# Four gate rows by way of DRAM instead of TensorE, and a written order at the end of the first MLP

## The chip, the cores and the metric

The kernel runs on one core of a Trainium2 chip. The metric is the device time of one execution in microseconds. A core has TensorE (PE, with its weight loads shown apart as PEld), VectorE (DVE), ScalarE (ACT) and GpSimd (POOL), which run their own instruction streams and wait for each other by semaphores, and SyncE (SP), whose stream here issues nearly all DMAs. DMAs move data between DRAM and the on-chip memory SBUF; matmul results arrive in the accumulator memory PSUM.

## The reference

Two layers of a diffusion backbone over 512 latent tokens and 256 context tokens, width 1024, hidden width 4096. Layer 0 mixes tokens by pooling, layer 1 by attention; each layer has an MLP with squared ReLU. Cut to what matters here:

```python
def ada_mods(cond, w, b):
    m = (jax.nn.silu(cond) @ w + b)[..., None, :]
    return jnp.split(m, N_MOD, axis=-1)
...
    for i in range(DEPTH):
        last = i == DEPTH - 1
        sh1, sc1, gt1, sh2, sc2, gt2 = ada_mods(c, w_ada[i], b_ada[i])
        csh1, csc1, cgt1, csh2, csc2, cgt2 = ada_mods(c_ctx, w_ada[i], b_ada[i])
        ...
        x = x + gt1 * rms_norm(y_lat, g_mix_post[i])
        m_lat = sq_relu_mlp(modulate(rms_norm(x, g_mlp_pre[i]), sh2, sc2), w_mlp_in[i], w_mlp_out[i])
        x = x + gt2 * rms_norm(m_lat, g_mlp_post[i])
        if not last:
            ctx = ctx + cgt1 * rms_norm(y_ctx, g_mix_post[i])
            ...
            ctx = ctx + cgt2 * rms_norm(m_ctx, g_mlp_post[i])
    return x
```

A gate, `gt1` or `gt2`, is one vector of 1024 numbers for all latent tokens and another for all context tokens. The kernel multiplies it with the gain of the norm behind it and applies it to rows of tokens.

## The kernel before

Tokens lie in six row tiles of 128: tiles 0 to 3 are latent, 4 and 5 context. Matmul operands are split into a high and a low float32r part, and a product is three matmuls (high by high, high by low, low by high).

**Two layouts of a gate.** The modulations come out as columns: number 128k + p of a vector sits in partition p, column k. The rows of tokens need the vector along the free axis, the same in all 128 partitions: the tile `gate`, [128, 2, 1024], slot 0 for latent rows and slot 1 for context rows. There are six such turns of a column into a row: one in two halves (`gate_half`) and one whole (`gate_rows`) early in layer 0, two in `before0`, one in the attention and one behind the last MLP. `gate_cols` (line 363) makes the column by one small VectorE multiply. `gate_rows` (line 373) turns it with eight float32 matmuls of the broadcast column by the identity, each recorded as two, and two ScalarE copies of PSUM. `gate_diag` (line 383) splits the column into two parts, has VectorE multiply the identity by each ([128, 8, 128], into tiles named diag), and sums over partitions with four matmuls against a column of ones, then copies on ScalarE. PSUM tiles of both are named psg and come from the pool `psB` (four banks), which out-products and transposes use too.

**The first MLP** (`mlp0`, line 1074) runs over 16 groups of 256 hidden channels on all 768 tokens. From the third group, an in-product is done with seven block products instead of eight (`Seven`, line 854): chains 0 to 6 of twelve matmuls each in the PSUM tile psin, chain 4 with the sums S3 and T3, chain 6 last. Between chains, ACT copies a bank or VectorE adds one, and the next chain on that bank waits. Each group's out-product (`out_mm`, line 1028, PSUM tile pso) adds into the token rows. For the last two groups it is done together in `finish` (line 1063), row tile by row tile in the order 4, 5, 0, 1, 2, 3, with 24 matmuls a tile: 12 of the older group, 12 of the newer. `last0` (line 1405) puts the norm, gate, residual and next norm of each tile behind it, and `norm_pair` turns two tiles at a time with 16 transposes (PSUM tile psx) for the projections (psq) of the attention. The context pair 4 and 5 is the first to be turned.

**Around it.** `mid0` and `extra0` (lines 1249 and 1258) run between and in the groups and compute the other modulations, on VectorE. `before0` (line 1449), behind the last in-product, closes the pool of sums, opens the pool of resident rows in its place (`xr`, `gate`, `junk`, `xl`), makes the two gates of layer 0's MLP by `gate_diag` and reloads the six row tiles from the DRAM tile `spill`. In the attention's list of steps `gate_rows` for layer 1's first gate stands at 39.281; the second MLP (`mlp1`, line 1101) ends with `residents` again, reloads and `finish`, with `gate_diag` for the last gate at 5.1.

**What sets the order.** The tile framework schedules the program with a simulated timeline (line 38), so instructions of one engine are ordered by program order, readiness and simulated times; DMAs too. A list of steps with times (`Steps`) sets the program order. `pin` and `tc.add_manual_dep` with `ISSUE` add an edge without a semaphore: the first must be issued behind the second. Regions of SBUF are handed out by pools, so another set of tiles shifts addresses. DMAs are issued on SP in the scheduled order, and a DMA that waits holds those behind it.

Of the kernel before, what the change touches and what calls it, by code (L numbers as in the profile page):

```python
# [9 lines left out]
F32 = mybir.dt.float32  # L10
# [43 lines left out]
def backbone(ctx: ExitStack, tc, x, c, ctx_in, c_ctx, w_ada, b_ada, g_mix_pre, g_mix_post,  # L54
# [53 lines left out]
    def residents(stack):  # L108
        rows = Rows(stack)
        return rows, rows.gate, rows.junk  # L110
# [2 lines left out]
    psA = ctx.enter_context(tc.tile_pool(name="psA", bufs=2, space=PSUM))  # L113
    psB = ctx.enter_context(tc.tile_pool(name="psB", bufs=4, space=PSUM))
    spill = ctx.enter_context(tc.tile_pool(name="spill", bufs=1, space=bass.MemoryType.DRAM)).tile([P, NT, D], F32, name="spill")

    acc = const.tile([P, NT * D], F32, name="acc")
    ident = const.tile([P, P], F32, name="ident")
# [261 lines left out]
                pin(z, i == 0 and m == GT1)  # L380
            sc.copy(gate[:, ci, 512 * h:512 * h + 512], ps)

    def gate_diag(i, m, ci, to=None):
        to = ci if to is None else to
        gc = gate_cols(i, m, ci)
        gh = small.tile([P, 2, KT], F32R, tag="gh", name="gh", bufs=2)
        ve.tensor_copy(gh[:, 0, :], gc)
        ve.tensor_tensor(out=gh[:, 1, :], in0=gc, in1=gh[:, 0, :], op=ALU.subtract)
        dg = [tmp.tile([P, KT, P], F32R, tag="t", name="diag") for _ in range(2)]
        for z, d in enumerate(dg):  # L390
            ve.tensor_tensor(out=d, in0=ident.unsqueeze(1).broadcast_to([P, KT, P]),
                             in1=gh[:, z, :].unsqueeze(2).broadcast_to([P, KT, P]), op=ALU.mult)
        for h in range(2):
            ps = psB.tile([P, 512], F32, tag="b", name="psg")
            for z, d in enumerate(dg):
                te.matmul(ps, onesr[:, 0:1].broadcast_to([P, P]), d[:, 4 * h:4 * h + 4, :], start=(z == 0), stop=(z == 1))
            sc.copy(gate[:, to, 512 * h:512 * h + 512], ps)

    def gate_half(h):
        gc = sm_tile("gc")  # L400
# [23 lines left out]

    late = []

    def modulated_pair(t, i, s, hi, lo, works, wide, fine, on_act):
        if (i, s) == (0, 1):
            place = lambda z, ks: z.rearrange("p k (h q n) -> p k q h n", h=2, n=P)[:, ks, t // 2]
# [6 lines left out]
        for q in range(4):  # L436
            if not wide:
                ps = psB.tile([P, 2, 256], F32, tag="b", name="psx")
            elif q % 2 == 0:
                both = psA.tile([P, 4, 256], F32, tag="a", name="psx")  # L440
            if wide:
                ps = both[:, 2 * (q % 2):2 * (q % 2) + 2, :]
            for kk in range(2):
                k = 2 * q + kk
                for u in range(2):
                    te.transpose(ps[:, kk, u * P:(u + 1) * P], works[u][:, k * P:(k + 1) * P], ident)
            pss.append(ps)
        for q in range(4):
            h = works[q // 2][:, 512 * (q % 2):512 * (q % 2) + 512].rearrange("p (k n) -> p k n", n=256)
# [403 lines left out]

    class Seven:
        def __init__(self, products, hid):
            self.products = products
            self.a, self.ntok = (hH, hL), TOK
            self.hid = [z.rearrange("p (f n) -> p f n", n=TOK) for z in hid]

        def chain(self, bank, n, start, stop):  # L860
            (wH, wL), (aH, aL) = self.products[n]
            for k in range(4):
                for m, (w, a) in enumerate(((wH, aH), (wH, aL), (wL, aH))):
                    te.matmul(bank, w[k], a[k], start=start and k == 0 and m == 0, stop=stop and k == 3 and m == 2,
                              skip_group_check=True)
# [159 lines left out]

    pso = {}

    def out_mm(i, parts, t, cols=HALVES):
# [11 lines left out]
        seq = [(a, f, w) for (_, (hi, lo), (wH, wL)) in parts for f in range(2)  # L1040
               for a, w in ((hi, wH), (hi, wL), (lo, wH))]
        order = [(n, h) for n in range(len(seq)) for h in range(len(cols))]
        if len(parts) > 1:
            order.sort(key=lambda z: (z[0] >= (9 if cols == HALVES else 0), z[1]))
        for n, h in order:
            a, f, w = seq[n]
            te.matmul(pss[h][:, 0:cols[h][1]], a[:, f, ts_], w[:, f, cols[h][0]:sum(cols[h])],
                      start=(n == 0 and not seeded[t]), stop=(n == len(seq) - 1), skip_group_check=seeded[t])
        pso[t] = pss

    def out_ev(i, parts, t, cols=HALVES):
# [11 lines left out]
    def finish(i, parts, order, last, also=()):  # L1063
        st = Steps()
        for z in also:
            st.at(*z)
        for n, t in enumerate(order):
            cols = THIRDS if (i, t) == (1, NL - 1) else HALVES
            st.at(5.2 * n, out_mm, i, parts, t, cols)
            st.at(5.2 * n + 5.2, out_ev, i, parts, t, cols)  # L1070
            last(st, n, t)
        st.run()

    def mlp0(inner, hids, order, extra, mid, last, before_last):
# [7 lines left out]
        for g in range(NG - 1):  # L1082
# [11 lines left out]
            else:  # L1094
                for t in range(NT):
                    out_mm(0, [part], t)
                    out_ev(0, [part], t)
        before_last()
        finish(0, [part, (NG - 1, inner.hid, wo_)], order, last)

    def mlp1(inner, last):
        nonlocal xr, gate, junk
# [66 lines left out]
        for p in range(NG // 2 - 1):  # L1169
# [29 lines left out]
            inner = inner_of(2 * p + 2)  # L1199
            if p == 1:  # L1200
                ada_fin(1, GT2, parts[1], 1)
        whole = lambda n: tuple(z.rearrange("p (f n) -> p f n", f=2) for z in (home[n], home[n + 1]))
        half_ = lambda n: (home[n][:, 0:1024], home[n][:, 1024:2048])
        wo_ = []
# [20 lines left out]
                add(m7_, m7_, m5)  # L1225
        closing.close()
        xr, gate, junk = residents(ctx)
        for t in range(NL):
            sy.dma_start(xr[:, t], spill[:, t])
        finish(1, [(NG - 2 + q, last_[q].hid, wo_[q]) for q in range(2)], range(NL), last, ((5.1, gate_diag, 1, GT2, 0),))  # L1230

    dual = [(0, GT2, 2), (1, SC1, 2), (1, SH1, 2)]
    lone = [(1, m, 1) for m in (GT1, SC2, SH2)]
# [359 lines left out]
    def attention(st, base, unit_t):  # L1593
# [127 lines left out]
```

## Time and profile before

| | before |
|---|---|
| median of 3 executions | 1157.09 us (1157.08 to 1157.51) |
| the profiled execution | 1157.33 us |
| its span | 1155.2 us |
| PE busy | 1134.3 us (98%), 6026 matmuls |
| PE weight loads busy | 979.8 us (85%) |
| DVE busy | 938.0 us (81%), 1551 instructions |
| ACT busy | 644.8 us (56%), 1150 instructions |
| POOL busy | 74.4 us (6%), 82 instructions |
| DMA | 152.08 MB, mean 132 GB/s |

The span goes from the first to the last instruction; the time of an execution holds 2.1 us more. Matmuls are pipelined and their ends are modelled, so a matmul of 128x512 is recorded with a length of 392 ns though in a run of many one starts every 0.23 us. Helpers record every operation, so that almost all lines read L68, and groups are told apart by the names of tiles: output, then inputs. "Idle before, releaser" is the time in which an engine stood still before an instruction and what ended it.

### The profile page before, as it was taken

To read this page: it belongs to the slowest core of one execution; us is meant where nothing else is said; L and a number is where in the kernel's file an instruction comes from. 1 tells how busy PE (TensorE), PEld (TensorE's weight loads), DVE (VectorE), ACT (ScalarE), POOL (GpSimd) and SP (SyncE) were. 2 spreads that over 40 slices of the span, in tenths; PEclk is the share of its full clock that TensorE was granted. 3 is DMA by queue.
4 is the path that set the end of the run, shared out by engine and by line. 5 is a ranking of instruction groups with operands and counts; after the bars stand their busy time and mean duration, and the time that the engine had idled before them with its cause. 6 is when DMAs were issued, how large, how long until landed. Compare 5 with 4: busy or idle time off the path is not lost.

```text
span 1155.2 us, 15680 instructions
## 1 busy us (share of the span) xinstructions
PE 1134.3 (98%) x6026; PEld 979.8 (85%) x6026; DVE 938.0 (81%) x1551; ACT 644.8 (56%) x1150; POOL 74.4 (6%) x82
## 2 busy tenths in 40 slices
PE   6999999999999999999999999999999999999998
PEld 5579889998899988998888889988988888888886
DVE  5798488889989898998778698978887779778876
ACT  6476655555435434555786378863876436534524
POOL 3040000000000000000231312100000000000000
PEclk9999999999999999999999999999999999999999
DMA  9992233244434444344442200145244224314303
GB/s 355 398 390 99 74 109 110 80 140 146 146 109 146 146 147 146 109 146 146 187 142 99 84 1 20 34 134 208 82 146 146 79 68 146 109 40 144 109 28 118
DMA packets 95305, 152.08 MB, mean 132 GB/s; under 512 B 2896, under 2 KB 68224, under 8 KB 95232
## 3 DMA queue, kind: packets, MB, share of 16 engines
q1 hardware_dynamic: 95136, 151.07, 37.8%
q8 instruction: 47, 0.77, 0.3%
q14 instruction: 26, 0.21, 0.1%
q10 hardware_dynamic: 96, 0.02, 0.0%
HBM read 141.65 MB, written 9.44 MB: 131 GB/s over the span
## 4 chain that ended last, share of the span: by engine, by line
PE 94%; DMA 3%; ACT 2%; DVE 1%; issue 0%; POOL 0%; DVEq 0%; SPq 0%; ACTq 0%
PE pso L68 36%; PE psin L68 35%; PE psq L68 7%; PE psy L68 4%; PE po L68 3%; PE pss L68 3%; DMA raw<-in_w_ada 2%; PE pspt L68 1%; PE psada L68 1%; PE pspool L68 1%; PE psx L68 1%; PE psg L68 1%; ACT ra L68 0%; DMA xr<-in_ctx 0%; DMA gate<-in_band 0%; ACT xr L68 0%
## 5 line engine op out<-in xcount | busy, mean ns | idle before, releaser
L68 PE MATMUL pso<-units,rb 128*128 128x512 f32 x1152 | 277.3, 392 | 0.0
L68 PEld LDWEIGHTS pso<-units,rb 128*128 128x128 f32 x1152 | 214.9, 188 | 41.7
L68 DVE TENSOR_TENSOR acc<-acc,pso 128x512 f32<-128x512 f32 x192 | 128.3, 680 | 61.5 <-PE pso L68 61.4
L68 DVE SCALAR_TENSOR_TENSOR rows<-raw,cond,rows 128x256 f32<-128x256 f32 x280 | 123.4, 483 | 0.9
L68 PE MATMUL psin<-ra 128*128 128x512 f32 (+1 forms) x424 | 112.4, 369 | 0.6 <-ACT work L68 0.6
L68 PE MATMUL psin<-ra,rb 128*128 128x512 f32 (+1 forms) x384 | 101.6, 360 | 0.0
L68 DVE TENSOR_TENSOR units<-raw,units 128x1024 fp32r<-128x1024 f32 (+2 forms) x69 | 82.4, 1203 | 13.8 <-ACT units L68 13.7
L68 ACT CAST units<-raw 128x1024 fp32r<-128x1024 f32 (+2 forms) x71 | 70.7, 1019 | 41.0 <-PE pso L68 21.8
L68 PE MATMUL psin<-rb,ra 128*128 128x384 f32 (+1 forms) x324 | 90.6, 356 | 0.0
L68 PEld LDWEIGHTS psin<-ra 128*128 128x128 f32 x424 | 77.8, 188 | 12.3 <-ACT work L68 1.0
L68 ACT ACTIVATE work<-psin 128x512 f32<-128x512 f32 (+3 forms) x66 | 36.0, 551 | 84.6 <-PE psin L68 82.4
L68 PE MATMUL psin<-ra,units 128*128 128x384 f32 x432 | 82.6, 336 | 0.4 <-ACT psin L68 0.4
L68 PE MATMUL pso<-units,pairs 128*128 128x512 f32 x336 | 82.3, 389 | 0.0
L68 PEld LDWEIGHTS psin<-ra,units 128*128 128x128 f32 x432 | 76.4, 188 | 3.2 <-ACT psin L68 0.5
L68 PEld LDWEIGHTS psin<-ra,rb 128*128 128x128 f32 x384 | 66.7, 189 | 11.5 <-issue 0.8
L68 PEld LDWEIGHTS pso<-units,pairs 128*128 128x128 f32 x336 | 63.1, 188 | 13.1
L68 PE MATMUL psin<-sums,units 128*128 128x384 f32 x336 | 63.6, 336 | 0.0
L68 PEld LDWEIGHTS psin<-rb,ra 128*128 128x128 f32 x324 | 58.6, 188 | 5.5
L68 ACT COPY acc<-pso 128x512 f32<-128x512 f32 x68 | 38.5, 592 | 40.1 <-PE pso L68 39.9
L68 PEld LDWEIGHTS psin<-sums,units 128*128 128x128 f32 x336 | 59.0, 188 | 1.3
L68 ACT CAST rb<-raw 128x2048 fp32r<-128x2048 f32 (+2 forms) x18 | 25.8, 1431 | 58.3 <-PE pso L68 55.8
L68 ACT ACTIVATE work<-work 128x768 f32<-128x768 f32 (+1 forms) x50 | 41.4, 831 | 28.8 <-DVE work L68 28.3
(226 smaller groups left out, 2118.9 us busy)
## 6 DMA issues: line engine op xcount, KB each, us to landing
raw<-in_w_ada SPq DMA_DIRECT2D x48, 1024.0 KB, 5.4
raw<-in_w_mlp_in SPq DMA_DIRECT2D x32, 1024.0 KB, 5.3
raw<-in_w_mlp_out SPq DMA_DIRECT2D x32, 1024.0 KB, 6.0
raw<-in_w_qkv SPq DMA_DIRECT2D x6, 1024.0 KB, 5.1
spill<-xl SPq DMA_DIRECT2D x8, 512.0 KB, 5.5
xl<-spill SPq DMA_DIRECT2D x8, 512.0 KB, 7.1
raw<-in_w_o SPq DMA_DIRECT2D x4, 1024.0 KB, 5.0
xl<-in_x SPq DMA_DIRECT2D x4, 512.0 KB, 5.5
```

The lines of the kernel that those rows point to most:

```text
L68: z = made(*args, **kw)
```

## The change

A DRAM tile `grows` holds four rows of 1024. `gate_away` makes the column as before and writes it with one DMA into a row, one run of 4 bytes for each number; `gate_back` reads a row into all 128 partitions of a slot of `gate`. They replace all three calls of `gate_diag` and the late one of `gate_rows`. The columns of layer 0's two MLP gates are written in groups 7 and 8 of the first MLP, that of layer 1's first gate in `before0`, that of the last gate in the fourth pass of the second MLP; the rows come back in `before0`, at 36.95 in the attention's list, and in front of the last reloads. A tile `phase2` that nothing uses stands for the column parts of `gate_diag`.

Besides, edges set the order on TensorE at the end of the first MLP: of tile 4's out-products (first in order) the first four have no edge, the next four follow chain 4 of the last in-product, the others and all of tile 5 follow chain 6; and the last eight out-products of tile 2 (fifth in order) follow the last transpose of the context pair.

```diff
+    rows_out = ctx.enter_context(tc.tile_pool(name="grows", bufs=1, space=bass.MemoryType.DRAM)).tile([4, D], F32, name="grows")
...
-    def gate_diag(i, m, ci, to=None):
...
+    row_of = {(0, GT2, 0): 0, (0, GT2, 1): 1, (1, GT1, 0): 2, (1, GT2, 0): 3}
+
+    def gate_away(i, m, ci):
         gc = gate_cols(i, m, ci)
...
+        with nc.allow_non_contiguous_dma(reason="one column of gates for each partition"):
+            sy.dma_start(rows_out[row_of[i, m, ci]].rearrange("(k p) -> p k", p=P), gc)
+
+    def gate_back(i, m, ci):
+        sy.dma_start(gate[:, ci, :], rows_out[row_of[i, m, ci]].partition_broadcast(P))
...
-                    te.transpose(ps[:, kk, u * P:(u + 1) * P], works[u][:, k * P:(k + 1) * P], ident)
+                    turned_[t] = te.transpose(ps[:, kk, u * P:(u + 1) * P], works[u][:, k * P:(k + 1) * P], ident)
...
-        for n, h in order:
+        for m, (n, h) in enumerate(order):
             a, f, w = seq[n]
-            te.matmul(pss[h][:, 0:cols[h][1]], a[:, f, ts_], w[:, f, cols[h][0]:sum(cols[h])],
-                      start=(n == 0 and not seeded[t]), stop=(n == len(seq) - 1), skip_group_check=seeded[t])
+            z = te.matmul(pss[h][:, 0:cols[h][1]], a[:, f, ts_], w[:, f, cols[h][0]:sum(cols[h])],
+                          start=(n == 0 and not seeded[t]), stop=(n == len(seq) - 1), skip_group_check=seeded[t])
+            if len(parts) > 1 and behind_chains and t == order_[4] and m >= 16:
+                tc.add_manual_dep(z.ins, turned_[NL].ins.name, ISSUE, reason="row order")
+            if len(parts) > 1 and behind_chains and t in order_[0:2]:
+                lead = t == order_[0] and n < 4
+                if t == order_[0] and n < 2:
+                    continue
+                tc.add_manual_dep(z.ins, behind_chains[0 if lead else 1].ins.name, ISSUE, reason="row order")
...
+        order0.extend(order)
+        behind_chains.extend(inner.ends[z] for z in (4, 6))
         finish(0, [part, (NG - 1, inner.hid, wo_)], order, last)
+        del behind_chains[:]
...
+            if p == 3:
+                gate_away(1, GT2, 0)
...
+        gate_back(1, GT2, 0)
         for t in range(NL):
             sy.dma_start(xr[:, t], spill[:, t])
-        finish(1, [(NG - 2 + q, last_[q].hid, wo_[q]) for q in range(2)], range(NL), last, ((5.1, gate_diag, 1, GT2, 0),))
+        finish(1, [(NG - 2 + q, last_[q].hid, wo_[q]) for q in range(2)], range(NL), last, )
...
+        if g in (7, 8):
+            gate_away(0, GT2, g - 7)
...
+        gate_away(1, GT1, 0)
+        small.tile([P, 2, KT], F32R, tag="gh", name="phase2", bufs=2)
         S["held"].close()
         xr, gate, junk = residents(held[1])
-        gate_diag(0, GT2, 0)
-        gate_diag(0, GT2, 1)
+        gate_back(0, GT2, 1)
+        gate_back(0, GT2, 0)
...
-        at(39.281, gate_diag if False else gate_rows, 1, GT1, 0)
+        at(36.95, gate_back, 1, GT1, 0)
```

More of the change, by code (lines that the diff above doesn't have):

```diff
@@ L381, in gate_rows @@
             sc.copy(gate[:, ci, 512 * h:512 * h + 512], ps)
-    def gate_diag(i, m, ci, to=None):
-        to = ci if to is None else to
+    row_of = {(0, GT2, 0): 0, (0, GT2, 1): 1, (1, GT1, 0): 2, (1, GT2, 0): 3}
+    def gate_away(i, m, ci):
         gc = gate_cols(i, m, ci)
[L386 to L397, printed above, removed]
+        with nc.allow_non_contiguous_dma(reason="one column of gates for each partition"):
+            sy.dma_start(rows_out[row_of[i, m, ci]].rearrange("(k p) -> p k", p=P), gc)
+    def gate_back(i, m, ci):
+        sy.dma_start(gate[:, ci, :], rows_out[row_of[i, m, ci]].partition_broadcast(P))
     def gate_half(h):
@@ L425, in backbone @@
     late = []
+    turned_ = {}
     def modulated_pair(t, i, s, hi, lo, works, wide, fine, on_act):
@@ L855, in __init__ @@
         def __init__(self, products, hid):
-            self.products = products
+            self.products, self.ends = products, {}
             self.a, self.ntok = (hH, hL), TOK
@@ L863, in chain @@
                 for m, (w, a) in enumerate(((wH, aH), (wH, aL), (wL, aH))):
-                    te.matmul(bank, w[k], a[k], start=start and k == 0 and m == 0, stop=stop and k == 3 and m == 2,
-                              skip_group_check=True)
+                    self.ends[n] = te.matmul(bank, w[k], a[k], start=start and k == 0 and m == 0,
+                                             stop=stop and k == 3 and m == 2, skip_group_check=True)
         def run(self, between=None):
@@ L1026, in backbone @@
     pso = {}
+    order0, behind_chains = [], []
     def out_mm(i, parts, t, cols=HALVES):
@@ L1041, in out_mm @@
                for a, w in ((hi, wH), (hi, wL), (lo, wH))]
+        order_ = order0
         order = [(n, h) for n in range(len(seq)) for h in range(len(cols))]
```

## The prediction

> **What bounds the kernel now.** I read the chain that ended last first, because its shares say which engine the end hangs on; then the table by stretches, to see where that engine has gaps; then the merged chain round the four gates. Engine letters are those of the page; a chain row is start, length, engine, tile and count.
>
> ```profile
> PE 94%; DMA 3%; ACT 2%; DVE 1%; issue 0%; POOL 0%; DVEq 0%; SPq 0%; ACTq 0%
> 112.00:543.00 431.00, 430.88 (x2186) 386.95 (x2184) 369.52 (x674) 217.45 (x325) 0.00 (x0) 1.00 0.38 125
> 543.00:557.00 14.00, 13.72 (x69) 12.32 (x70) 9.93 (x12) 8.18 (x13) 0.00 (x0) 1.00 0.74 262
> 830.00:1130.00 300.00, 300.00 (x1331) 248.21 (x1331) 236.65 (x273) 152.43 (x195) 0.00 (x0) 1.00 0.31 105
> ```
>
> The stretch rows give length, then busy time of PE, weight load, DVE, ACT, POOL, the granted clock, the DMA share and GB/s. TensorE is busy for all of both MLPs at a granted clock of 1.00, and 94% of the chain is its. So a matmul taken out shortens the kernel by its own length wherever something else is ready behind it, and work taken from DVE or ACT brings nothing by itself.
>
> The gates themselves are the tile psg. First the end of the first MLP, with two of them:
>
> ```profile
> 539.14 3.51 PE psin L68 x20
> ...
> 542.73 0.47 ACT psin L68
> ...
> 543.25 4.45 PE psin L68 x24
> 547.70 0.46 PE psg L68 x2
> 548.16 2.11 PE psin L68 x12
> ...
> 550.30 0.73 PE psg L68 x2
> 551.03 2.26 PE psin L68 x12
> 553.29 0.46 PE psg L68 x2
> 553.75 2.73 PE pso L68 x12
> 556.48 0.46 PE psg L68 x2
> 556.94 19.09 PE pso L68 x84
> 576.03 0.22 PE psx L68 x2
> 576.25 5.49 PE pso L68 x24
> 581.74 1.53 PE psx L68 x14
> ```
>
> The reader sees the last seven-product in-product (psin) with its chains in the order 3 and 5, 4, 6, the out-products of the last two groups (pso), and gate matmuls in between. One out-product costs 19.09/84 = 0.227 us; a gate matmul costs 0.46/2 = 0.23. PE has two holes: from 539.14 + 3.51 = 542.65 to 543.25 (0.60, waiting for ACT's copy of the bank), and from 548.16 + 2.11 = 550.27 to 551.03, where chain 6 waits for VectorE's add; of these 0.76 us the gate matmuls fill 0.46, so 0.30 is idle.
>
> The other two gates:
>
> ```profile
> 766.49 0.22 PE psg L68 x2
> ...
> 767.55 1.56 PE psg L68 x14
> 769.11 38.56 PE psy L68 x168
> ...
> 1132.01 0.93 PE psg L68 x4
> 1132.94 16.53 PE pso L68 x84
> ```
>
> **The change part by part.**
>
> **Gates of layer 0's MLP.** Eight psg matmuls go: 4 x 0.46 = 1.84 us, all on the chain. The two holes stay unless filled. The edges say with what: the first four out-products of row tile 4 (n below 2, two halves) get no edge and may go into the hole at 542.65, the next four follow chain 4, everything else of tiles 4 and 5 follows chain 6. Four take 4 x 0.227 = 0.91 us, more than either hole, so 0.60 + 0.30 = 0.90 us of idle time is used by work that has to be done anyway. Behind chain 6 there remain 24 - 8 = 16 out-products of the older group, 16 x 0.227 = 3.6 us; before, 12 and four psg covered 553.29 to 556.94, 3.65 us. The cover for ACT's and DVE's work on the last hidden tile is the same, so nothing new is late there. Without the filling the holes cost 0.9, and with 0.46 of cover gone behind chain 4 up to 0.46 more. Gain: 1.84 + 0.90 = 2.74; from 1.4 to 2.8.
>
> **Attention's gate.** Two psg groups go, 0.22 + 1.56 = 1.78 us. Behind them stands psy, whose operands of the first row tile are there: DVE wrote the low part at 766.04 (row below). I take the full 1.78; if psy were still held, 0.
>
> ```profile
> 765.62 0.43 DVE L68 TENSOR_TENSOR ra<-po,ra 128x256 fp32r<-128x256 f32 x1 [1.53 <-ACT ra L68]
> ```
>
> **The last gate.** 0.93 us of psg at 1132.01, with out-products on both sides: gain 0.93. The tail behind the last out-product is unchanged.
>
> **DVE, ACT.** The six diag multiplies on DVE and the eight gate copies on ACT go; both engines have gaps in those stretches (DVE 9.93 of 14.00 us), so I count nothing.
>
> **Context rows' turns.** The 16 turns (psx) now stand in front of the last eight out-products of tile 2, the fifth in order. Before, tile 2 starts at 576.25, behind two turns of 0.22; now at about 576.03 - 2.74 = 573.3, and its 16th out-product ends at 573.3 + 16 x 0.227 = 576.9. The turns need the normalised tile 5:
>
> ```profile
> 560.88 1.37 DVE L68 TENSOR_TENSOR acc<-acc,pso 128x512 f32<-128x512 f32 x2 [3.64 <-PE pso L68]
> 566.42 5.20 POOL L68 TENSOR_TENSOR rb<-raw,rb 128x2048 fp32r<-128x2048 f32 x1 [1.28 <-ACT rb L68]
> 577.75 1.14 ACT L68 ACTIVATE acc<-xr,rs 128x1024 f32<-128x1024 f32 x1
> ```
>
> Before, it is ready at 577.75 + 1.14 = 578.89. If that chain shifts by the whole 2.74 it is ready at 576.15 and nothing waits; if not at all, PE stands 2.0 us. Its first link is the eviction of tile 4, at 560.88, behind which ACT and then POOL's split follow in line. Tile 4's out-products now end at about 553.2 + 28 x 0.227 = 559.6 (chain 6 ends near 553.2; then the 16 and its own last 12), so the eviction comes some 1.1 us sooner, not 2.74, because the slots gained before it go to tile 5. By that 578.89 - 1.1 = 577.8 against 576.9: an estimate of 0.9. I take 0.7 of loss. An earlier turn brings nothing by itself: behind 576 PE is packed.
>
> **DMAs.** Added are four writes of a column (1024 runs of 4 bytes) and four rows read back to 128 partitions (128 runs of 4 KB, 512 KB). No row shows the former. The nearest are loads with as many runs, 5.3 us, and the copy of the pool scale, a broadcast of 512 KB (issued at 12.31, used at 22.65, with other loads ahead of it in a full queue).
>
> ```profile
> raw<-in_w_mlp_in SPq DMA_DIRECT2D x32, 1024.0 KB, 5.3
> 12.31 2.25 SPq L583 DMA_DIRECT2D pscale<-in_pool_scale  x1
> ...
> 22.65 4.37 POOL L68 TENSOR_TENSOR raw<-raw,pscale 128x512 f32<-128x512 f32 x3 [8.20 <-DMA pscale<-in_pool_scale]
> 556.00:558.00 2.00, 2.00 (x11) 1.62 (x10) 0.96 (x1) 1.32 (x3) 0.00 (x0) 1.00 1.02 410
> 549.14 0.37 SPq L146 DMA_DIRECT2D raw<-in_w_qkv  x1
> xr<-spill SPq DMA_DIRECT2D x2, 512.0 KB, 5.9
> 562.16 1.29 DVE L68 TENSOR_TENSOR work<-acc,gate 128x512 f32<-128x512 f32 x2
> ```
>
> The gate region is free when chain 4 has read the sums, about 550. Behind the weight load of 549.14 two gates take 1 MB at 410 GB/s, 2.6 us; before, the first of the row loads landed 5.9 us after its issue at 550.3, so the gates land about 556 and the rows 2.6 us later than before. The gate is first read at 562.16 before, perhaps at 561 now: 5 us of room. By the pool scale's 10.3 us from issue to use it would be 560.6, still in time for the first, 562 for the second. SP stands for 0.4 to 2.3 us for each issue; behind it wait the six row loads and the next weight chunk, read later still. The last gate goes out with the row loads:
>
> ```profile
> 1122.59 1.77 SPq L1229 DMA_DIRECT2D xl<-spill  x4
> 1133.36 0.69 DVE L68 TENSOR_TENSOR work<-acc,gate 128x512 f32<-128x512 f32 x1 [0.16 <-ACT gate L68]
> ```
>
> Some 10 us for a transfer of 512 KB. Cost taken: nothing, with the rivals holding the other end. The column writes depend on modulations finished long before, and stand in the loops, where DMA is busy for 0.38 of the time. SP sends them between weight loads, and a load right behind one is late by up to its length.
>
> **The sum.** 2.74 + 1.78 + 0.93 - 0.7 = 4.75 us. The profiled execution took 1157.33 us with a span of 1155.2; minus 4.75 that is 1152.6. The median shown is 1157.09, 0.24 below, so **1152.3 us**.
>
> **The rivals.**
>
> *Weight loads come late behind 4-byte writes; slower.* Place: the rounds of the first MLP in which a column is written. There a load has little room:
>
> ```profile
> 304.17 0.37 SPq L146 DMA_DIRECT2D raw<-in_w_mlp_in  x1
> ...
> 309.43 1.05 ACT L68 CAST units<-raw 128x1024 fp32r<-128x1024 f32 x1 [1.17 <-DMA raw<-in_w_mlp_in]
> 310.63 1.22 DVE L68 TENSOR_TENSOR units<-raw,units 128x1024 fp32r<-128x1024 f32 x1
> ...
> 316.15 1.05 PE L68 MATMUL psin<-ra,units 128*128 128x384 f32 x5
> ```
>
> ACT waits for it, and the chain that uses it starts 316.15 - 311.85 = 4.3 us after its low part is written (310.63 + 1.22). A write that holds the rings 5.3 us costs 1.0; one of twice that costs 10.6 - 4.3 = 6.3. With two such rounds (three columns are written there, a load right behind two) 12.6: 1152.3 + 12.6 = 1164.9. It beats the gain and 2.3 us more from 7.1 us in all, 3.5 a write, thus from a hold of 7.8 us. For it: the run of 4 bytes is unlike anything in the trace. Against: 62% of the loop's DMA time is free, and the columns are ready early. The Trainium skill, "DMA: Bandwidth & Descriptors", section "Rules for kernel authors", says that a non-contiguous last dimension becomes one descriptor per element; its "Specifications" says that below 512 B the engine reads, modifies and writes. By that a column write might take twice a load of equal runs, an estimate by that page, and this rival would hold; no run here shows such a write yet. Chance 0.09.
>
> *The DMA's wait takes the gate's place.* Gates and rows land some 9 us late (a gate at 565, read at 561) because the broadcast of one row runs slower than 410 GB/s. The evictions of tiles 0 to 3 then hold the four psB banks and PE waits with them, for some 4 us: 1156.3. For: nothing in the trace reads one DRAM row 128 times at this place. Against: the pool scale is such a broadcast, and its 10.3 us include the loads ahead of it. Chance 0.11.
>
> *The row order stalls PE.* If the 5.20 us split on POOL slips between tile 5's reciprocal root and its use, the turns wait for about all of it: 5.2 - 0.7 = 4.5 more, 1156.8. Chance 0.11; the rest of the small delays is in the forecast.
>
> *The order does nothing that the gap did not.* The scheduler already fills 542.65, or the holes stay: 0.9 back, and psy waits for half of the 1.78 at 767: 1152.3 + 1.8 = 1154.1. Chance 0.13.
>
> **How the numbers follow.** Forecast 0.56 (1149.7 to 1153.5; the order of all engines comes from a simulated timeline, and I allow 2.6 us below the sum for a rearrangement that happens to fit better, 1.2 above it for one that fits worse); the rivals 0.09, 0.11, 0.11, 0.13. The range from 1149.3 to 1156.9 leaves out the slow case and the far ends. About 0.2%, 2.3 us, can be told from no change, so faster is below 1154.8: forecast 0.56, nearly all of the last rival 0.12, a third of the two waiting ones 0.08, together 0.76. Same: the rest of those, 0.14. Slower 0.10.
>
> **What would show it.** Right: no psg matmuls after 60 us; out-products between chains 2 and 3 and between 4 and 6; the 84-run's start near 554 to 557 with 24 instead of 12 done; psy near 764; TensorE busy time down by about 4.5 us. Wrong: DVE waiting for a DMA of gate; PE waiting before psx near 577; ACT or DVE waiting longer for in_w_mlp_in than the 1.17 us shown; psg time gone but idle time on PE up by as much.

## The result and the profile after

The changed kernel takes 1154.98 us at the median of 11 executions (1153.73 to 1156.23), the kernel before 1157.26 in the 11 measured beside it (1156.76 to 1157.94). The ratio is 0.9979, 95% interval 0.9970 to 0.9988: a gain of 2.28 us where the prediction had 4.75. The profiled execution is the fastest of the eleven, 1153.73 us, so what its trace shows lost is less than what the median lost.

The page of the changed kernel, the busy time of PE and the shares of the chain that ended last:

```profile
PE 1129.6 (98%) x5998; PEld 975.8 (85%) x5998; DVE 925.5 (80%) x1539; ACT 641.0 (56%) x1142; POOL 75.3 (7%) x82
...
PE 85%; ACT 5%; DVE 5%; DMA 3%; issue 1%; SPq 0%; POOL 0%; DVEq 0%; ACTq 0%
```

PE's work fell by 1134.3 - 1129.6 = 4.7 us, as the prediction had it. But the span fell by only 1155.2 - 1151.9 = 3.3, and PE's share of the chain went from 94% to 85%: other engines and DMAs now hold it up in places. Where, the table by stretches says (columns as in the prediction: length, busy time of PE, weight load, DVE, ACT, POOL, clock, DMA share, GB/s), first after, then one row of before that was not shown yet:

```profile
112.00:543.00 431.00, 430.23 (x2166) 386.00 (x2165) 368.46 (x668) 217.40 (x324) 0.00 (x0) 1.00 0.38 123
543.00:557.00 14.00, 14.00 (x89) 12.85 (x88) 5.46 (x8) 7.01 (x10) 0.00 (x0) 1.00 0.70 238
557.00:589.00 32.00, 30.59 (x144) 24.99 (x143) 20.61 (x29) 27.26 (x63) 13.85 (x11) 1.00 0.52 199
```

```profile
557.00:589.00 32.00, 32.00 (x151) 26.56 (x150) 22.22 (x27) 26.07 (x59) 12.52 (x11) 1.00 0.31 121
```

The holes among the last chains are gone (14.00 of 14.00). Two new ones have come: 0.8 us in the loop of the first MLP, where only writes were added (though the scheduler orders TensorE anew there from 319 on), and 1.41 us between 557 and 589. The timeline of PE after, at the end of the first MLP (start, length, form, count, and in brackets the idle time ahead and what ended it):

```profile
543.99 1.19 PE L68 MATMUL pso<-units,rb 128*128 128x512 f32 x4
...
551.26 1.09 PE L68 MATMUL pso<-units,rb 128*128 128x512 f32 x4
552.18 2.27 PE L68 MATMUL psin<-ra 128*128 128x384 f32 x12
554.29 22.19 PE L68 MATMUL pso<-units,rb 128*128 128x512 f32 x97
576.32 0.38 PE L68 MATMUL psx<-ident,acc 128*128 128x128 f32 x2
576.46 1.87 PE L68 MATMUL pso<-units,rb 128*128 128x512 f32 x7
578.16 1.69 PE L68 MATMUL psx<-ident,acc 128*128 128x128 f32 x14
579.61 7.73 PE L68 MATMUL pso<-units,rb 128*128 128x512 f32 x32
587.17 0.38 PE L68 MATMUL psx<-ident,acc 128*128 128x128 f32 x2
588.97 3.02 PE L68 MATMUL psq<-rb,ra 128*128 128x512 f32 x12 [1.41 <-DVE work L68]
```

The written order is there: four out-products between chains 2 and 3, four between 4 and 6, the rest behind. The turns (psx) wait for nothing; psq does, for VectorE to read out a bank of psB. The loop's loss is this row of PE:

```profile
353.46 1.83 PE L68 MATMUL psin<-sums,units 128*128 128x384 f32 x9 [0.77 <-ACT psin L68]
```

It begins near 342 with a late load. SyncE issues three of the four columns in the loop (that of `before0` was moved up into it): two at 292, one at 324. Its issues in the changed kernel, and the DMA table of a window round the last three of them (tile, queue, count, KB each, us from issue to landing):

```profile
292.14 2.70 SPq L389 DMA_DIRECT2D grows<-gc  x2
...
323.65 0.37 SPq L147 DMA_DIRECT2D raw<-in_w_mlp_out  x1
324.07 0.46 SPq L389 DMA_DIRECT2D grows<-gc  x1
333.11 0.37 SPq L147 DMA_DIRECT2D raw<-in_w_mlp_in  x1
```

```profile
raw<-in_w_mlp_in SPq DMA_DIRECT2D x1, 1024.0 KB, 8.7
grows<-gc SPq DMA_DIRECT2D x1, 4.0 KB, 13.4
```

A column of 4 KB lands 13.4 us after its issue, at 337.4, and the load issued 9.04 us behind it lands after 8.7 us, where it took 5.3 before. The two columns of 292 land after 12.5 us, and the load issued 11.97 us behind them takes 6.6 instead of 5.2. ScalarE is the first to feel it, after and before:

```profile
341.84 1.05 ACT L68 CAST units<-raw 128x1024 fp32r<-128x1024 f32 x1 [5.46 <-DMA raw<-in_w_mlp_in]
```

```profile
338.58 1.05 ACT L68 CAST units<-raw 128x1024 fp32r<-128x1024 f32 x1 [2.05 <-DMA raw<-in_w_mlp_in]
```

Starts of PE's rows at six places give the account; "placed" is the run e5_writes_later below:

| start of, us | before | after | placed |
|---|---|---|---|
| the loop's last psada | 542.57 | 543.75 | 542.52 |
| psq, behind the first MLP | 588.62 | 588.97 | 587.73 |
| first pss of the attention | 665.52 | 665.20 | 664.26 |
| psy<-ra, behind the attention's gate | 771.75 | 769.63 | 768.70 |
| psada<-part, in the second MLP | 909.85 | 907.73 | 906.80 |
| last pso run | 1148.58 | 1145.48 | 1144.55 |

After against before: 1.18 lost in the loop; from there to pss 1.50 gained; 1.80 in the attention; and 0.98 from psada<-part to the end, which is the last gate's time alone, so the column written near 990 in the second MLP cost nothing.

### The profile page after: what moved, and what is told of

Its sections match the earlier page's. It is cut to its first block, busy times and chain, and to the rows that moved or that the text cites. A ratio compares the mean times of both kernels' runs of the same rounds, so it can differ in the third digit from the quotient of the medians.

```text
span 1151.9 us, 15610 instructions
## 1 busy us (share of the span) xinstructions
PE 1129.6 (98%) x5998; PEld 975.8 (85%) x5998; DVE 925.5 (80%) x1539; ACT 641.0 (56%) x1142; POOL 75.3 (7%) x82
## 4 chain that ended last, share of the span: by engine, by line
PE 85%; ACT 5%; DVE 5%; DMA 3%; issue 1%; SPq 0%; POOL 0%; DVEq 0%; ACTq 0%
PE psin L68 32%; PE pso L68 30%; PE psq L68 7%; PE psy L68 4%; PE po L68 3%; PE pss L68 3%; DMA raw<-in_w_mlp_in 2%; PE pspt L68 1%; PE psada L68 1%; ACT junk L68 1%; PE pspool L68 1%; DVE acc L68 1%; DVE rows L68 1%; PE psx L68 1%; DMA raw<-in_w_ada 1%; ACT ra L68 1%
```

## The experiments

Theory at the start: the columns' writes hold up the loads behind them until they complete. Rival: the loop is later because the changed program is scheduled otherwise. Times are medians; each ratio is to the kernel before, run on the same chip.

**1. No writes.**

```diff
-        with nc.allow_non_contiguous_dma(reason="one column of gates for each partition"):
-            sy.dma_start(rows_out[row_of[i, m, ci]].rearrange("(k p) -> p k", p=P), gc)
+        return gc
...
-        sy.dma_start(gate[:, ci, :], rows_out[row_of[i, m, ci]].partition_broadcast(P))
+        sy.dma_start(gate[:, ci, :], g_mlp_post[i].partition_broadcast(P))
```

> As the changed kernel, but the four column writes are left out and the four rows are read from a row of the input, so the gates' values are not the reference's; TensorE's order is that of the changed kernel to the instruction. Theory (the writes hold SyncE's queue until they complete, 12.5 and 13.4 us after their issue, and the loads of the first MLP behind them land late: 8.7 us where it was 5.3): the mlp_in load issued near 333 lands in about 5.3 us again, the 5.46 us wait of the CAST for in_w_mlp_in near 342 falls to about 2, the last psada moves back by about 1.4 us to near 542.5, and the time is about 1153.6, 1.4 below the changed kernel's 1154.98. Rival (the loss in the loop comes of the changed schedule, not of the writes): the load lands in 8.7 us all the same or the wait stands, and the time is within 0.4 of 1155.0.

1153.55 us (6 runs), ratio 0.9970 (0.9958 to 0.9981). The load near 333 lands in 5.3 us, ScalarE's wait is 2.04, the last psada starts at 542.67, and PE has no hole between 300 and 400. The theory holds, the rival falls: the order of TensorE, VectorE, ScalarE and GpSimd is that of the changed kernel.

**2. The writes alone, on the kernel before.** `gate_away` and its three places are added, `gate_diag` stays.

> The kernel before with the four column writes added, whose rows nobody reads; gates by diagonals as before. Theory (writes hold the queue): slower than before by the same 1.4 us, about 1158.6 against 1157.2, with a longer wait for in_w_mlp_in behind the write near 324. Rival (schedule): within 0.4 of the kernel before, 1157.2.

1165.16 us (5 runs), ratio 1.0074 (1.0061 to 1.0088): 8.1 us slower, which neither theory had. The added instructions made the scheduler order PE anew from the middle of the loop on, and one of the holes is this:

```profile
357.80 2.37 PE L68 MATMUL psin<-sums,units 128*128 128x384 f32 x12 [1.73 <-ACT psin L68]
```

```profile
raw<-in_w_mlp_in SPq DMA_DIRECT2D x1, 1024.0 KB, 5.4
grows<-gc SPq DMA_DIRECT2D x1, 4.0 KB, 12.7
```

The write is slow here too, but the load near it takes its usual time. It was issued at 341.02, when the write of 324.94 had landed (337.6); the load of 304.73, issued while two writes were under way, takes 6.8. So the run prices another order and says nothing of the writes' price.

**3. Without any written order.** `behind_chains` is never filled, so none of the edges is set.

```diff
-        behind_chains.extend(inner.ends[z] for z in (4, 6))
```

> The changed kernel without the written order of the last in-products' neighbours and of tile 5's turns: the rows still go through DRAM, the out-products stand as the kernel's own order puts them. If TensorE bounds the end of the first MLP, as the prediction had it (0.90 us of two holes filled, 0.7 lost to the turns): about 0.2 slower at most than the changed kernel with the turns' loss taken off, and psq starts about as late. If ScalarE's chain of row norms bounds the stretch from 561 to 589 (the theory after the trace): what counts is when tile 4's rows are evicted (561.1 in the changed kernel); without the order they are evicted 1 to 2 us later or earlier as the 16 products before chain 4 fall, and the time moves by that whole amount: 1154 to 1157. The same wait for in_w_mlp_in near 342 as in the changed kernel (5.5 us) by both.

1165.16 us (5 runs), ratio 1.0067 (1.0055 to 1.0080): 10.2 above the changed kernel. The forecast of at most some 2 us was far off; runs 10 and 11 take the order apart.

**4. The writes on ScalarE's queue.**

```diff
-            sy.dma_start(rows_out[row_of[i, m, ci]].rearrange("(k p) -> p k", p=P), gc)
+            sc.dma_start(rows_out[row_of[i, m, ci]].rearrange("(k p) -> p k", p=P), gc)
```

> The changed kernel with the four column writes issued on ScalarE's queue in place of SyncE's; the rows are read as in it. Theory (what is held is SyncE's queue, by the writes' completion): the loads of the first MLP are not behind the writes any more, the wait for in_w_mlp_in near 342 falls to about 2 us, and the time is about 1153.6, plus what ScalarE loses by issuing (2.7 us of issue for the pair, which stands between evictions: up to 1 us if it does not fall in a gap). If the hold is of the sixteen DMA engines and not of the queue, the load lands in 8 to 9 us as in the changed kernel and the time is 1155 or more. Rival (schedule): 1155.0.

1154.69 us (11 runs), ratio 0.9979 (0.9970 to 0.9988), as the changed kernel. Its DMA table in the same window:

```profile
raw<-in_w_mlp_in SPq DMA_DIRECT2D x1, 1024.0 KB, 8.4
grows<-gc ACTq DMA_DIRECT2D x1, 4.0 KB, 13.3
```

The load on SyncE's queue is as late behind a write on ScalarE's. So it isn't SyncE's queue that is held but something that both queues share. The Trainium skill, "DMA: Bandwidth & Descriptors", section "Issuing engines are not separate DMA queues", says that DMAs of all issuing engines run on the same 16 DMA engines and interleave. The first half agrees with 8.4 against 8.7. Of the second, this is what the changed kernel's trace shows round the load of 333.11: the packets recorded from 327 to 329, and stretches behind them (DMA share in the last column but one).

```profile
DMA packets 1143, 0.36 MB, mean 180 GB/s; under 512 B 1056, under 2 KB 1056, under 8 KB 1143
```

```profile
332.00:334.00 2.00, 2.00 (x11) 1.70 (x11) 1.05 (x3) 0.00 (x0) 0.00 (x0) 1.00 0.00 0
334.00:336.00 2.00, 2.00 (x12) 1.83 (x11) 0.69 (x1) 0.21 (x1) 0.00 (x0) 1.00 0.19 4
336.00:338.00 2.00, 2.00 (x12) 1.82 (x11) 0.76 (x2) 0.38 (x1) 0.00 (x0) 1.00 0.55 58
```

```profile
334.00:336.00 2.00, 2.00 (x12) 1.79 (x11) 0.69 (x1) 0.06 (x1) 0.00 (x0) 1.00 0.76 191
336.00:338.00 2.00, 2.00 (x12) 1.86 (x11) 0.61 (x2) 0.53 (x1) 0.00 (x0) 1.00 0.96 332
```

The last fence is the kernel before, its load issued at 333.25. After, the tiny packets are all recorded by 329, 8 us before the write lands. The load's packets start at 334 in both kernels, so the load isn't shut out; but they are slow until the write has landed. By the rows from 336 to 338, 0.55 x 2 us x 16 engines for 116 KB is about 0.16 us for a run of 1 KB, where 0.96 x 2 us x 16 for 664 KB is 0.05 before (estimates). What slows them, and why a write lands so long after its last packet, no row shows.

**5. The three writes behind the loop's last mlp_in load.** They stand in `before0`; four buffers for gc instead of two, one phase2 instead of two. Only SyncE's order differs from the changed kernel.

```diff
+        in_load[g] = load_[0]
...
+        if (i, m) != (1, GT2):
+            tc.add_manual_dep(d.ins, in_load[NG - 1].ins.name, ISSUE, reason="row order")
...
-            gate_away(0, GT2, g - 7)
...
+        for z in ((0, GT2, 0), (0, GT2, 1), (1, GT1, 0)):
+            gate_away(*z)
```

> The changed kernel with the three column writes of the first MLP issued right behind its last mlp_in load (near 519), ahead of a stretch of some 11 us without a transfer; the orders of the four other engines are the changed kernel's to the instruction. Theory (a write of 1024 four-byte runs costs time only where a load is due before it lands): the three still land in 12 to 14 us, the loads of the loop land in 5.2 to 7.3 us as before, the wait for in_w_mlp_in near 342 falls to about 2 us, PE has no hole between 300 and 400, and the time is that of the run without the writes, about 1153.5 (1.4 below the changed kernel's 1154.98). Rival (the writes cost the same wherever they stand): about 1155.0, with a late mlp_out or w_qkv load near 536 to 545.

1152.70 us (5 runs, 1152.63 to 1152.89), ratio 0.9962 (0.9948 to 0.9976). This is faster than both kernels: 4.35 under the kernel before, 2.28 under the changed one, and all five executions lie under all eleven of the changed kernel. Against the kernel before on each one's own chip the two gains differ by 2.07. SyncE's issues, and the DMA table:

```profile
519.01 0.37 SPq L147 DMA_DIRECT2D raw<-in_w_mlp_in  x1
519.43 4.68 SPq L392 DMA_DIRECT2D grows<-gc  x3
536.13 0.37 SPq L147 DMA_DIRECT2D raw<-in_w_mlp_out  x1
```

```profile
raw<-in_w_mlp_out SPq DMA_DIRECT2D x1, 1024.0 KB, 10.0
grows<-gc SPq DMA_DIRECT2D x3, 4.0 KB, 16.9
```

Of three writes together two landings are recorded, after 14.9 and 18.9 us, longer than expected, and the mlp_out load behind them takes 10.0. ScalarE waits 3.10 us for it at 546.24. But its weights are used by PE only behind chain 6, near 553, and PE has no hole there. The writes have not become cheaper; they stand where a late load costs nothing.

One thing stays open: run 1, which has no write at all, is 0.85 slower than this run at the median, though in the traces its TensorE is level with run 5's to the last out-products (1144.40 against 1144.55).

**8. The same writes in an eighth of the runs**, sent together with 5, 6 and 7.

```diff
-            sy.dma_start(rows_out[row_of[i, m, ci]].rearrange("(k p) -> p k", p=P), gc)
+            sy.dma_start(rows_out[row_of[i, m, ci]].rearrange("(p k) -> p k", p=P), gc)
```

> The changed kernel with each column write sent as 128 runs of 32 bytes (the gates then stand in the row in another order, so the four gates' values are not the reference's); same places, same orders on all engines. Theory (the number of runs, 1024 of four bytes, sets the 12.5 to 13.4 us until a write lands and frees the rings): with an eighth of the runs it lands in 2 to 4 us, the mlp_in load near 333 lands in about 5.3 us, and the time is about 1153.5, as without writes. Rival (a small write to DRAM takes its 12 us whatever the number of its runs): it lands in 10 us or more and the time is about 1155.0.

1152.70 us (5 runs), ratio 0.9963 (0.9950 to 0.9975).

```profile
raw<-in_w_mlp_in SPq DMA_DIRECT2D x1, 1024.0 KB, 5.2
grows<-gc SPq DMA_DIRECT2D x1, 4.0 KB, 4.6
```

The same 4 KB in 128 runs of 32 bytes land in 4.6 us, somewhat more than the expected 2 to 4 (the two sent together near 293 in 6.9 at the median), and the load is on time. So it is the cut into 1024 runs of 4 bytes that makes the price. The number of runs alone is not it, since a load of 1024 runs of 1 KB lands in 5.3; count and length were changed together here.

**6. The hole of 1.41 us: a split moved ahead.** Theory: ScalarE's chain of row norms from 561 on sets it.

```diff
-            st.at(5.5, lambda: split(*raw0[0], True, False, True))
+            st.at(0.1, first_split)
...
+        for z in hid_cast:
+            tc.add_manual_dep(a.ins, z.ins.name, ISSUE, reason="row order")
```

> The changed kernel with one 128x2048 CAST on ScalarE (1.90 us, the high part of the first w_qkv chunk) and its low part on GpSimd moved ahead of tile 4's row norms, into ScalarE's idle stretch between the last hidden CAST and tile 4's eviction (4.5 us). Theory (ScalarE's chain of norms, seeds and casts from 561 to 588 sets when the psB bank of the first psq is read out, so the 1.41 us hole ahead of psq is ScalarE's): the hole falls below 0.2 us, and the time is about 1153.6, 1.4 below the changed kernel's 1154.98. Rival (TensorE or a wait behind psq, such as the 0.53 us of units behind GpSimd, takes the place of the hole): the hole goes or shrinks and the time stays within 0.4 of 1155.0.

1156.80 us (11 runs), ratio 0.9997 (0.9988 to 1.0006): 1.8 slower than the changed kernel, and the hole is 1.41 still. The theory falls in this form. The move has a cost on VectorE. GpSimd's low part of the split and two rows of VectorE in this run, then the pair of the second row in the changed kernel:

```profile
560.17 4.67 POOL L68 TENSOR_TENSOR rb<-raw,rb 128x2048 fp32r<-128x2048 f32 x1 [484.53 <-ACT rb L68]
```

```profile
562.02 1.37 DVE L68 TENSOR_TENSOR acc<-acc,pso 128x512 f32<-128x512 f32 x2 [2.80 <-PE pso L68]
563.30 2.08 DVE L68 TENSOR_TENSOR work<-acc,gate 128x512 f32<-128x512 f32 x1
```

```profile
562.39 1.28 DVE L68 TENSOR_TENSOR work<-acc,gate 128x512 f32<-128x512 f32 x2
```

Of the pair that reads two SBUF tiles, the first takes 2.08 us instead of half of 1.28, and ends at 565.38, 0.54 behind GpSimd's subtraction (564.84). In the kernel before, such a product that starts at 566.98 takes 5.18 and ends 0.54 behind the subtraction of 566.42 (5.20 us). So by these rows one product waits until GpSimd is done, and the one behind it is as fast as ever. The pair that reads PSUM and SBUF is not slowed. The Trainium skill, "GPSIMD Engine Reference", section "1. Specifications", says that GpSimd shares its SBUF interfaces with VectorE and contends with instructions that have two SBUF inputs; these rows agree. Tile 5's turns now wait 0.64 us for its rows, and counted from the last psada psq starts 1.88 later than in the changed kernel, about what the run is slower.

**7. Both edits**, 5 and 6.

> Both edits: writes behind the last mlp_in load, and the first w_qkv chunk's split ahead of the row norms. If the two losses are apart in time and both are real, the gains add: 1154.98 - 1.4 - 1.4, about 1152.2, which is the time the prediction forecast. If only the writes cost time: about 1153.5. If neither edit reaches the path: 1155.

1154.65 us (11 runs), ratio 0.9978 (0.9970 to 0.9987): 1.95 above run 5, as run 6 is above the changed kernel. Gain and loss add up; the hole is 1.41 again. Runs 6 and 7 differ in the writes' place alone and were measured on one chip: 2.15 us. The profiled execution of run 6 is its median, and there about the whole price stands in the loop, where the last psada starts at 544.66, in run 7 at 542.40.

**9. One cast from ScalarE to GpSimd, on run 5.** In the changed kernel and in runs 1 and 4 to 8 psq starts 8.45 or 8.46 us after ScalarE's first modulation behind the turns, and ScalarE has no gap in between; in the kernel before, with fewer casts ahead of the read-out, it is 5.91.

```diff
-            st.at(31.302, lambda: split(*raws[0], False, False, True, 2))
+            st.at(31.302, lambda: split(*raws[0], False, True, True, 2))
```

> The run with the writes behind the last mlp_in load, with one of the three 128x512 CASTs units<-raw (0.63 us, 0.51 from start to start) that stand on ScalarE between the turns of tile 5 and the read-out of the bank that psq takes moved to GpSimd. Theory (the 1.41 us hole ahead of psq is ScalarE's work from the turns x14 to that read-out, 8.46 us from its first modulation to psq's start in every run so far, beside 7.9 us of products): the hole shrinks to about 0.9 and the time goes from 1152.70 to about 1152.2; PE's order behind psq differs a little. Rival (the hole is a fixed latency of the hand-over from the last product, 1.41 in all runs): it stays 1.41 and the time stays within 0.3 of 1152.7, or GpSimd's low parts come late for psq's products with units and the time grows by up to 1.

1153.05 us (5 runs), ratio 0.9964 (0.9951 to 0.9976).

```profile
587.54 3.01 PE L68 MATMUL psq<-rb,ra 128*128 128x512 f32 x12 [0.85 <-DVE work L68]
```

The hole shrinks by 0.56, as ScalarE's queue ahead of the read-out does. So it is ScalarE's work between the turns and the read-out, not a fixed hand-over. The time did not follow: PE's order behind psq changed too, and the first pss starts 0.3 later than in run 5.

**10. Run 5 without the written turns**: the two lines with `turned_[NL]` are left out.

> The same run without the written order of tile 5's turns; the out-products then stand 100, 2 turns, 12, 14 turns, 24. By the prediction (the written turns cost 0.7 us, because tile 5's rows come late for them): about 1152.0. By the theory that ScalarE needs 8.46 us from the turns to the read-out: the turns start some 1.3 to 2 us later, with 5.7 us of products behind them in place of 7.7, the hole ahead of psq grows from 1.41 to about 3, and the time is about 1154.3.

1157.36 us (11 runs), ratio 1.0001 (0.9992 to 1.0011). The whole gain is gone. PE, then VectorE, then all engines from 590 to 594 (columns as above):

```profile
590.08 4.51 PE L68 MATMUL psq<-rb,ra 128*128 128x512 f32 x12 [3.93 <-DVE work L68]
```

```profile
584.40 4.42 DVE L68 TENSOR_TENSOR ra<-acc,ra 128x512 fp32r<-128x512 f32 x3
588.74 0.68 DVE L68 TENSOR_TENSOR units<-raw,units 128x512 fp32r<-128x512 f32 x1
589.34 0.68 DVE L68 TENSOR_TENSOR work<-pso,gate 128x512 f32<-128x512 f32 x1
```

```profile
590.00:594.00 4.00, 3.92 (x11) 3.12 (x12) 3.91 (x7) 2.38 (x8) 0.55 (x1) 0.59 0.94 326
```

The hole grew by more than expected: the read-out (589.34) now stands on VectorE behind subtractions that take 4.42/3 = 1.47 us apiece instead of 0.6, beside GpSimd's of 581.87 to 588.3. Psq starts 2.35 later than in run 5. The rest is the clock: behind the hole, from 590 to 594, the granted clock is 0.59 (last row), and 4 us at 0.59 lose 0.41 x 4 = 1.6 us. By the first pss (668.02, in run 5 664.26) 3.76 is lost, and the two profiled executions differ by 3.74. In run 5 the clock is 1.00 behind its hole of 1.41.

**11. Run 5 without the edges round the chains**; the turns stay written.

> The run with the writes behind the last mlp_in load, without the written order of the out-products around the last chains; tile 5's turns stay written. TensorE then does 8 older out-products between chains 2 and 3, 16 ahead of chain 4 and none between 4 and 6, so none of the 24 is left behind chain 6. If the prediction's price holds (two holes of 0.90 us together that the order fills): 1152.7 + 0.9, about 1153.6. If the 24 older products are the cover behind chain 6 (in the run without any order TensorE stood 0.65 us ahead of chain 6 and 2.91 us behind it for the last hidden rows, and the evictions of tile 4 were as much later): 1152.7 + 4 to 6, about 1157.5.

1158.59 us (11 runs), ratio 1.0011 (1.0002 to 1.0020): 5.9 above run 5, the second of the two expectations.

```profile
549.20 3.83 PE L68 MATMUL pso<-units,rb 128*128 128x512 f32 x16
...
555.78 2.38 PE L68 MATMUL psin<-ra 128*128 128x384 f32 x12 [0.65 <-DVE work L68]
561.07 20.29 PE L68 MATMUL pso<-units,rb 128*128 128x512 f32 x81 [2.90 <-ACT rb L68]
```

```profile
562.00:566.00 4.00, 4.00 (x13) 3.11 (x12) 0.07 (x2) 0.00 (x0) 0.00 (x0) 0.57 1.02 413
```

The scheduler puts 8 and 16 older out-products ahead of the last chains. Then none is left behind chain 6, and PE stands 2.90 us for ScalarE's last hidden rows. Here too the hole is followed by a low clock: 0.57 from 562 to 566, which loses 0.43 x 4 = 1.7 us. With the holes, 0.65 + 2.90, that is 5.25 of the 5.9. The eleven executions fit this: they go from 1156.78 us at a mean clock of 0.999 to 1160.79 at 0.997. Run 3 has two such stretches, behind holes of 2.91 and 3.92.

**12. The written order on the kernel before**, with gates by diagonals: all edges of the change, none of its rows.

> The kernel before, gates by diagonals, with the whole written order of the change and without its rows. Up to the turns TensorE's order is that of before to the instruction; then 16 out-products, 14 turns and 32 out-products stand in place of 24, 14 and 24. If the order alone brings time (the gap that the prediction filled): below 1156.3. If it brings nothing without the rows, because TensorE had no hole there in the kernel before and the gates' matmuls stand between the chains already: within 0.6 of 1157.2. If the turns come before tile 5's rows are ready, or ScalarE's 8.46 us from the turns to the bank's read-out leave a hole: 1157.8 to 1158.6.

1158.82 us (11 runs), ratio 1.0014 (1.0005 to 1.0022): 1.55 slower than before.

```profile
590.30 3.02 PE L68 MATMUL psq<-rb,ra 128*128 128x512 f32 x12 [0.97 <-DVE work L68]
```

The edge of the turns alone brings nothing and costs the third case, slightly more than expected. It says nothing of the edges round the chains: the order up to the turns is that of the kernel before, with its idle 0.37 us ahead of chain 3, so with the gate matmuls in place the scheduler put no out-product among the chains.

## Why the prediction was right and wrong

**The DMAs, "Cost taken: nothing": wrong, and this is the step that failed.** It bounded a column's write by the loads with as many runs, 5.3 us, and let DMA time that is free in the loop hide it. The write takes 12.5 to 13.4 us, and free DMA time does not help a load that stands behind it. The price is 2.28 us by the medians of the changed kernel and run 5, 2.15 by runs 6 and 7, most of what is missing between 4.75 and 2.28. (Run 8 gives 2.28 again, run 1 only 1.43, and why is open.) This was the prediction's first rival, held at 0.09. Its estimate, that a write in 4-byte runs takes twice a load of equal runs, was near: 13.4 against 5.3. Whether it is so for the reason that the prediction gives is not shown: runs of 32 bytes, for which the same reason holds, land in 4.6. Its price, 12.6 us, was far too high: it set the load right behind the write, while loads follow 9 to 12 us later, so only the tail counts, 8.7 - 5.3 = 3.4 us on a load with some room. What it said would show it, a longer wait for in_w_mlp_in, is the row at 341.84.

**End of the first MLP, 2.74: right in mechanism, but not all kept.** The eight gate matmuls are gone and both holes are filled. The first hole was misread in part: 16 short psada matmuls stand in it, and the profile names 0.37 idle of the 0.60. But from the last psada to the first two turns the change gains what was forecast: 33.30 us before, 32.57 after with nine more out-products done, 9 x 0.227 = 2.04, together 2.77 (an estimate from these rows). The hole ahead of psq gives half of it back: 0.83 is left at psq, and to the first pss the changed kernel keeps 1.50 of the stage, run 5 keeps 1.21, against 2.74 - 0.7 = 2.04. "Without the filling the holes cost 0.9, and ... up to 0.46 more" was mis-sized: without the edges it is 5.9 (run 11), because the order that comes in their place uses up the cover behind chain 6, and the low clock behind that hole adds 1.7.

**The turns, 0.7 of loss: wrong in mechanism.** Tile 5 was ready and the turns waited for nothing. The loss is later and twice as large: 1.41 of PE at psq, because ScalarE's work from the turns to a bank's read-out, 8.46 us, is longer than PE's between them. "ACT: I count nothing" took gaps of the stretch as a whole for gaps at that place. "An earlier turn brings nothing by itself" is not settled: run 12, which adds the turns' edge to the kernel before, loses 1.55, and run 10, which takes it out of run 5, loses 4.7, but by VectorE's order and the clock behind a longer hole.

**The attention's gate, 1.78, and the last gate, 0.93: right.** 1.80 and 0.98 by the table. **Gates back in time: right.** In the changed kernel they land 6.6 us after their issue at the median, and VectorE's first read of a gate, at 562.39, waits for no DMA; the second rival fell. The third fell as well: the split on GpSimd (4.77 us from 567.06) was done before tile 5's root at 575.90, and the turns did not wait. The fourth fell: the order fills the holes, and psy did not wait.

With the writes placed apart (run 5) the same change brings 4.35 us, 1152.70, beside a forecast of 1152.3. In its trace the span is 1155.2 - 1151.0 = 4.2 us shorter: the stage at the end of the first MLP is 0.83 short of its term, and the terms of the attention and of the last gate hold.

## What to carry to other kernels

Ask of a transfer how many runs it has, how short they are and what is issued while it is under way, not how many bytes it moves or how idle the DMA engines are: put one of many tiny runs right behind the last load of a round, ahead of the longest stretch without one. Removing work also removes what held a scheduler's order in place, so look at the order of every engine before pricing the removal; an edit that reorders an engine, as in runs 2 and 10, is not a test of the thing edited. Look at the granted clock behind a hole before pricing the hole by its length. And where one engine's share says it has gaps, look whether it has one between the two events that matter.

## What the runs showed of the hardware

- 1024 runs of 4 bytes from SBUF to DRAM land 12.5 (median of two) to 13.4 us after their issue in the changed kernel and up to 14.6 in run 3, one or two in flight; with three, 14.9 and 18.9. 128 runs of 32 bytes land in 4.6 us alone. A 1 MB load issued 9 us behind the former takes 8.7 us instead of 5.3, from another issuing queue as well (8.4): its packets are few and slow until the write has landed. Issued after the landing it takes 5.4 (run 2).
- The profiled executions with holes of 2.9 to 3.9 us on TensorE (runs 3, 10 and 11) show a low granted clock behind them (in 10 and 11 means of 0.59 and 0.57 over 4 us, by estimate a loss of 1.6 and 1.7 us); behind holes of 1.41 us it stays 1.00. How long a hole it takes, no run shows.
- The 11 executions of the changed kernel spread over 2.5 us, the 5 of run 5 over 0.3; the 11 each of runs 6 and 7 over 2.3 and 1.1. But run 11 spreads over 4.0 with the writes placed apart, so the writes are not the only cause.
- A VectorE product or subtraction of two SBUF tiles of 128x512, 0.60 us from start to start alone, that starts beside a GpSimd subtraction can wait for its end: 2.08 us in run 6, 5.18 in the kernel before, both ending 0.54 behind GpSimd.
